# Queueing all loads of a convolution ahead of its stores, the last three as casting loads

## The chip, the cores and the metric

The kernel runs on one core of a Trainium2 chip. The metric is device time in microseconds (us), the median of several runs; the profiler's span of one execution, about 1.8 us shorter than the time of that same execution (127.3 us in one of 129.07 us), is used when stages are compared. All runs quoted with a verdict were in the fast state.

## The reference

A 3x3 convolution with padding 1, in fp32 in memory: 16 images of 64 channels and 64x64 pixels, 128 output channels.

```python
batch, c_in, h, w, c_out = 16, 64, 64, 64, 128
x_pad = np.pad(x, ((0, 0), (0, 0), (1, 1), (1, 1)))
output[b, co] += weight[co, ci, kh, kw] * x_pad[b, ci, kh:kh+h, kw:kw+w]   # over ci, kh, kw
```

The kernel must read 17.07 MB and write 33.55 MB.

## The kernel before

Two images form a pair: 2 x 64 channels fill 128 partitions. ScalarE casts the pair's fp32 input `xf` to fp16 (`xs`), GpSimd sums neighbouring rows (`ss`), TensorE makes three groups of products per block of 16 output rows, ScalarE copies the first group out of PSUM (`ut`), and VectorE adds it to the other two into the outputs `ot`. A pool named `big`, 16 KB per partition and buffer, serves inputs and outputs alike: a pair needs one buffer for `xf` and two for `ot`.

```python
psum = ctx.enter_context(tc.tile_pool(name="psum", bufs=8, space=bass.MemoryType.PSUM))
big = ctx.enter_context(tc.tile_pool(name="big", bufs=9))

def load(p):
    xf[p] = big.tile([128, H, W], F32, tag="big", name="xf")
    # ... nc.sync.dma_start(xf[p], x rows of pair p); pair 0 in four pieces

def outs(p):
    ots[p] = [big.tile([128, H // 2, 2, W], F32, tag="big", name="ot") for _ in range(2)]

for p in range(4):
    load(p)
outs(0)
# ... weights; casts and sums of pair 0
casts = {p: [[(p + 1, n)] for n in range(4)] for p in range(NP - 1)}   # pair p+1's casts during pair p
# ...
for p in range(NP):                       # NP = 8 pairs
    if p not in ots:
        outs(p)
    if p + 1 < NP:
        for lo in (0, 16):
            sums(nc.gpsimd, p + 1, xf[p + 1], lo, 16)
    for blk in range(4):
        U = group([(G1, None)])           # matmuls on ss
        # ScalarE: ut = copy of U (two tiles); then casts[p][blk]
        A = group([(G21, 1), (G0, -1)])   # matmuls on xs
        # VectorE: ots[p][b2][even rows] = A[b2] + ut[b2]
        Bt = group([(G01, 0), (G2, 2)])
        # VectorE: ots[p][b2][odd rows] = Bt[b2] + ut[b2]
        # after block 3 (pair 7: blocks 1 and 3): nc.sync.dma_start(out, ots[p][b2])
    if p < 4:
        load(p + 4)
        if p < 3:
            outs(p + 1)
```

Of the kernel before, what the change touches and what calls it, by code (L numbers as in the profile page):

```python
# [9 lines left out]
F16 = mybir.dt.float16  # L10


@with_exitstack
def kernel(
    ctx: ExitStack,
    tc: tile.TileContext,
    x: bass.AP,
    weight: bass.AP,
    out: bass.AP,
):  # L20
    nc = tc.nc
    B, CI, H, W = x.shape
    CO = weight.shape[0]
    assert H == 64 and W == 64 and CI == 64 and CO == 128 and B % 2 == 0
    NP = B // 2
    RB = 8

    keep = tc.keep_in_program_order
    x_rows = x.rearrange("b c h w -> (b c) h w")
    out_rows = out.rearrange("b co h w -> b co h w")  # L30
    w_flat = weight.rearrange("co ci kh kw -> co (ci kh kw)")

    const = ctx.enter_context(tc.tile_pool(name="const", bufs=1))
    psum = ctx.enter_context(tc.tile_pool(name="psum", bufs=8, space=bass.MemoryType.PSUM))
    xpool = ctx.enter_context(tc.tile_pool(name="xpool", bufs=3))
    big = ctx.enter_context(tc.tile_pool(name="big", bufs=9))
    spool = ctx.enter_context(tc.tile_pool(name="spool", bufs=3))
    upool = ctx.enter_context(tc.tile_pool(name="upool", bufs=4))




    w_raw = const.tile([CO, CI * 9], F32)
    nc.sync.dma_start(w_raw, w_flat)  # L44
    cuts = [(0, 18), (18, 34), (34, 50), (50, 64)]
    xf, xs = {}, {}

    def load(p):
        xf[p] = big.tile([128, H, W], F32, tag="big", name="xf")
        for lo, hi in cuts if p == 0 else [(0, H)]:  # L50
            keep(
                nc.sync.dma_start(
                    xf[p][:, lo:hi, :], x_rows[128 * p : 128 * p + 128, lo:hi, :]
                )
            )

    def cast(p, n):
        if p not in xs:
            xs[p] = xpool.tile([128, H, W], F16, tag="xs", name="xs")
        lo, hi = cuts[n]  # L60
        keep(nc.scalar.copy(xs[p][:, lo:hi, :], xf[p][:, lo:hi, :]))  # L61

    ots = {}

    def outs(p):
        ots[p] = [big.tile([128, H // 2, 2, W], F32, tag="big", name="ot") for _ in range(2)]

    for p in range(4):
        load(p)
    outs(0)  # L70
    ident = const.tile([128, 128], F16)
    make_identity(nc, ident)
    w16 = const.tile([CO, CI * 9], F16)
    keep(nc.vector.tensor_copy(w16, w_raw))  # L74


    ss = {}

    def sums(eng, p, src, lo, n):
        if p not in ss:  # L80
            ss[p] = spool.tile([128, H // 2, W], F16, tag="ss", name="ss")
        v = src.rearrange("p (j i) c -> p j i c", i=2)
        keep(
            eng.tensor_add(  # L84
                ss[p][:, lo : lo + n, :], v[:, lo : lo + n, 0, :], v[:, lo : lo + n, 1, :]
            )
        )


    Wt = const.tile([128, 5, 3, CO], F16)  # L90
    G0, G21, G1, G01, G2 = range(5)

    def wrow(i):
        return Wt[:, i, :, :].rearrange("p t c -> p (t c)")

    wps = {}
    for kh in (1, 2, 0):
        wp = psum.tile([128, 512], F32, tag="acc", name="wp")
        for k in range(3):
            t = 3 * kh + k  # L100
            for q in (0, 64):
                nc.tensor.matmul(wp[q : q + 64, k * CO : k * CO + CO], w16[:, t::9], ident)  # L102
        wps[kh] = wp[:, 0 : 3 * CO]
    keep(nc.scalar.copy(wrow(G1), wps[1]))  # L104
    sums(nc.vector, 0, xf[0], 0, RB)
    keep(nc.vector.tensor_sub(wrow(G21), wps[2], wrow(G1)))  # L106
    keep(nc.vector.tensor_sub(wrow(G01), wps[0], wrow(G1)))  # L107
    cast(0, 0)
    keep(nc.scalar.copy(wrow(G0), wps[0]))  # L109
    keep(nc.scalar.copy(wrow(G2), wps[2]))  # L110
    for n in range(1, 4):
        sums(nc.vector, 0, xf[0], RB * n, RB)


    casts = {p: [[(p + 1, n)] for n in range(4)] for p in range(NP - 1)}
    casts[0] = [[(0, 1)], [(0, 2), (0, 3)], [(1, 0), (1, 1)], [(1, 2), (1, 3)]]
    casts[NP - 1] = [[], [], [], []]

    for p in range(NP):
        if p not in ots:  # L120
            outs(p)
        if p + 1 < NP:
            for lo in (0, 16):
                sums(nc.gpsimd, p + 1, xf[p + 1], lo, 16)
        for blk in range(4):
            j0 = blk * RB

            def group(wi_rows):

                tiles = [  # L130
                    psum.tile([128, RB, W], F32, tag="acc", name="acc") for _ in range(2)
                ]
                n = 3 * len(wi_rows)
                i = 0
                for wi, off in wi_rows:
                    for kw in (1, 0, 2):
                        c_lo, c_hi = max(0, 1 - kw), min(W, W + 1 - kw)
                        for b2 in range(2):
                            p0 = 64 * b2
                            lo, hi = j0, j0 + RB  # L140
                            if off is None:
                                rhs = ss[p][p0 : p0 + 64, lo:hi, c_lo + kw - 1 : c_hi + kw - 1]
                            else:
                                while 2 * lo + off < 0:
                                    lo += 1
                                while 2 * (hi - 1) + off > H - 1:
                                    hi -= 1
                                first = 2 * lo + off
                                last = 2 * (hi - 1) + off
                                rhs = xs[p][  # L150
                                    p0 : p0 + 64,
                                    first : last + 1 : 2,
                                    c_lo + kw - 1 : c_hi + kw - 1,
                                ]
                            nc.tensor.matmul(  # L155
                                tiles[b2][:, lo - j0 : hi - j0, c_lo:c_hi],
                                Wt[p0 : p0 + 64, wi, kw, :],
                                rhs,
                                start=i == 0,
                                stop=i == n - 1,  # L160
                            )
                        i += 1
                return tiles

            U = group([(G1, None)])
            us = []
            for b2 in range(2):
                ut = upool.tile([128, RB, W], F32, tag="ut", name="ut")
                keep(nc.scalar.copy(ut, U[b2]))  # L169
                us.append(ut)  # L170
            for q, n in casts[p][blk]:
                cast(q, n)
            A = group([(G21, 1), (G0, -1)])
            for b2 in range(2):
                nc.vector.tensor_add(ots[p][b2][:, j0 : j0 + RB, 0, :], A[b2], us[b2])  # L175
            Bt = group([(G01, 0), (G2, 2)])
            for b2 in range(2):
                nc.vector.tensor_add(ots[p][b2][:, j0 : j0 + RB, 1, :], Bt[b2], us[b2])  # L178
            parts = {3: (0, 64)} if p < NP - 1 else {1: (0, 32), 3: (32, 64)}
            if blk in parts:  # L180
                lo, hi = parts[blk]
                for b2 in range(2):
                    keep(nc.sync.dma_start(
                        out_rows[2 * p + b2, :, lo:hi, :],
                        ots[p][b2].rearrange("p j i c -> p (j i) c")[:, lo:hi, :],
                    ))

        if p < 4:
            load(p + 4)
            if p < 3:  # L190
                outs(p + 1)


# [1 line left out]
_INS = ['x', 'weight']  # L195
# [26 lines left out]
```

## Time and profile before

| | before |
|---|---|
| time | 128.8 us (128.3 to 129.51, 3 runs) |
| span | 127.3 us |
| TensorE ends | 113 us |
| last data packet ends | 125.9 us |
| moved | 50.63 MB at 428 GB/s in the steady stretch |

A page shows the span in 40 equal slices of about 3.2 us. A digit is the busy share of an engine in tenths, 9 meaning full. Waits are listed as "engine, what it was about to write, line <- releaser: total us, times, longest". The lines that carry the reading of before stand in the prediction below.

### The profile page before, as it was taken

The page shows a single profiled execution, that of the slowest core. Times are in us where ns is not written, and L with a number is a line of the kernel's source. Part 1 is how long each engine was busy: PE and PEld are TensorE (multiplying, and loading weights), DVE is VectorE, ACT ScalarE, POOL GpSimd, SP SyncE. Part 2 cuts the span into 40 slices and gives each one's busy share as a digit, 9 for nine tenths or more (in the row PEclk, how much of TensorE's full clock was granted, in tenths as well). Part 3 has the DMA queues.
Part 4 walks back from the last instruction along what each step waited for, and adds up shares of the span by engine and source line. Part 5 has one row for each costly group of instructions (what it writes and reads, how often), then busy time and mean ns, then how long its engine had stood idle before and what let it go on. Part 6 is the DMA issues. An engine that isn't in the chain of part 4 may idle for free.

```text
span 127.3 us, 2440 instructions
## 1 busy us (share of the span) xinstructions
PE 108.7 (85%) x978; PEld 60.2 (47%) x978; DVE 84.2 (66%) x135; ACT 67.2 (53%) x100; POOL 33.5 (26%) x20
## 2 busy tenths in 40 slices
PE   0489999999999999999999999999999999990000
PEld 0334555564556655565556555555555555540000
DVE  0286777875778677777778678777877778773000
ACT  4283889866566646664666466666666633330000
POOL 2000399695000670009400390007600000000000
PEclk9999999999999999999999999999999999999555
DMA  4999999999999999999999999999999999999970
GB/s 127 300 427 438 432 427 427 391 417 412 350 422 355 430 427 409 443 427 417 427 432 438 422 417 422 453 422 427 422 417 448 422 422 427 450 391 430 425 337 18
DMA packets 4330, 50.77 MB, mean 399 GB/s; under 512 B 480, under 2 KB 480, under 8 KB 1120
## 3 DMA queue, kind: packets, MB, share of 16 engines
q1 hardware_dynamic: 4320, 50.63, 95.7%
q8 instruction: 7, 0.11, 0.3%
q14 instruction: 3, 0.02, 0.0%
HBM read 17.07 MB, written 33.55 MB: 398 GB/s over the span
## 4 chain that ended last, share of the span: by engine, by line
PE 75%; ACT 5%; issue 4%; DMA 4%; DVE 2%; DVEq 0%; SPq 0%
PE acc L155 75%; DMA xf<-in_x_dram 4%; ACT xs L61 3%; ACT ut L169 2%; DVE ot L175 1%; DVE ss L84 1%; DVE ot L178 0%; DVEq L217 0%; SPq L44 0%; DVEq L175 0%
## 5 line engine op out<-in xcount | busy, mean ns | idle before, releaser
L155 PE MATMUL acc<-xs,Wt 64*128 64x504 f16 (+3 forms) x768 | 102.9, 380 | 0.3
L155 PEld LDWEIGHTS <-Wt 64*128 64x128 f16 x960 | 59.1, 96 | 49.6 <-issue 6.5
L175 DVE TENSOR_TENSOR ot<-acc,ut 128x512 f32<-128x512 f32 x64 | 41.2, 686 | 24.4 <-PE acc L155 23.1
L169 ACT COPY ut<-acc 128x512 f32<-128x512 f32 x64 | 34.4, 590 | 40.9 <-issue 37.1
L84 POOL TENSOR_TENSOR ss<-xf 128x1024 f16<-128x1024 f32 x14 | 32.8, 2362 | 57.2 <-DMA xf<-in_x_dram 55.8
L155 PE MATMUL acc<-ss,Wt 64*128 64x504 f16 (+1 forms) x192 | 41.4, 384 | 1.4 <-DVE ss L84 1.4
L178 DVE TENSOR_TENSOR ot<-acc,ut 128x512 f32<-128x512 f32 x64 | 41.1, 684 | 0.7 <-PE acc L155 0.7
L61 ACT CAST xs<-xf 128x1024 f16<-128x1024 f32 (+2 forms) x32 | 33.5, 1058 | 0.8 <-DMA xf<-in_x_dram 0.8
L102 PE MATMUL wp<-ident,w 128*64 128x128 f16 x18 | 1.3, 328 | 4.2 <-DVE w L74 4.2
L84 DVE TENSOR_TENSOR ss<-xf 128x512 f16<-128x512 f32 x4 | 2.8, 690 | 2.7 <-DMA xf<-in_x_dram 2.7
L102 PEld LDWEIGHTS <-w 128*64 128x64 f16 x18 | 1.1, 209 | 4.2 <-DVE w L74 4.2
L74 DVE CAST w<-w_raw 128x576 f16<-128x576 f32 x1 | 0.5, 460 | 3.6 <-DMA w_raw<-in_weight_dram 3.6
L104 ACT CAST Wt<-wp 128x384 f16<-128x384 f32 x1 | 0.5, 479 | 2.8 <-PE wp L102 2.8
L104 ACT ACT_TABLE_LOAD x1 | 1.3, 1283 | 0.7 <-PEq L206 0.7
L109 ACT CAST Wt<-wp 128x384 f16<-128x384 f32 x1 | 0.5, 478 | 0.5 <-DVE Wt L107 0.5
L106 DVE TENSOR_TENSOR Wt<-wp,Wt 128x384 f16<-128x384 f32 x1 | 0.6, 552 | 0.0
L107 DVE TENSOR_TENSOR Wt<-wp,Wt 128x384 f16<-128x384 f32 x1 | 0.5, 549 | 0.0
L110 ACT CAST Wt<-wp 128x384 f16<-128x384 f32 x1 | 0.5, 485 | 0.0
masks.py:199 POOL TENSOR_SCALAR_AFFINE_SELECT ident<-ident 128x128 f16<-128x128 f16 x1 | 0.3, 292 | 0.1
masks.py:197 POOL MEMSET ident<- 128x128 f16 x1 | 0.2, 204 | 0.3 <-POOLq L206 0.3
L206 POOL MEMSET const-float32-0.0<- 128x1 f32 x1 | 0.1, 98 | 0.2 <-issue 0.2
L206 POOL MEMSET const-bfloat16-1.0<- 128x1 bf16 x1 | 0.1, 101 | 0.0
(2 smaller groups left out, 0.2 us busy)
## 6 DMA issues: line engine op xcount, KB each, us to landing
out_dram<-ot SPq DMA_DIRECT2D x14, 2048.0 KB, 13.6
xf<-in_x_dram SPq DMA_DIRECT2D x7, 2048.0 KB, 19.5
out_dram<-ot SPq DMA_DIRECT2D x4, 1024.0 KB, 10.6
xf<-in_x_dram SPq DMA_DIRECT2D x2, 512.0 KB, 6.1
xf<-in_x_dram SPq DMA_DIRECT2D x1, 576.0 KB, 4.9
xf<-in_x_dram SPq DMA_DIRECT2D x1, 448.0 KB, 7.1
w_raw<-in_weight_dram SPq DMA_DIRECT2D x1, 288.0 KB, 2.9
```

The source lines that it names most:

```text
L61: keep(nc.scalar.copy(xs[p][:, lo:hi, :], xf[p][:, lo:hi, :]))
L74: keep(nc.vector.tensor_copy(w16, w_raw))
L84: eng.tensor_add(ss[p][:, lo : lo + n, :], v[:, lo : lo + n, 0, :], v[:, lo : lo + n, 1, :])
L102: nc.tensor.matmul(wp[q : q + 64, k * CO : k * CO + CO], w16[:, t::9], ident)
L104: keep(nc.scalar.copy(wrow(G1), wps[1]))
L106: keep(nc.vector.tensor_sub(wrow(G21), wps[2], wrow(G1)))
L107: keep(nc.vector.tensor_sub(wrow(G01), wps[0], wrow(G1)))
L109: keep(nc.scalar.copy(wrow(G0), wps[0]))
L155: nc.tensor.matmul(tiles[b2][:, lo - j0 : hi - j0, c_lo:c_hi], Wt[p0 : p0 + 64, wi, kw, :], rhs, start=i == 0, stop=i == n - 1,)
L169: keep(nc.scalar.copy(ut, U[b2]))
L175: nc.vector.tensor_add(ots[p][b2][:, j0 : j0 + RB, 0, :], A[b2], us[b2])
L178: nc.vector.tensor_add(ots[p][b2][:, j0 : j0 + RB, 1, :], Bt[b2], us[b2])
```

## The change

The intent is that no store stands in front of a load. Pairs 0 to 4 are loaded as fp32 into eight buffers shared with the outputs, and pairs 5 to 7 by loads that cast on the way, issued from GpSimd into fp16 tiles of their own, so that ScalarE's casts for them vanish.

```diff
-    big = ctx.enter_context(tc.tile_pool(name="big", bufs=9))
+    big = ctx.enter_context(tc.tile_pool(name="big", bufs=8))
+    NH = 5
...
+    def load_cast(p):
+        xs[p] = xpool.tile([128, H, W], F16, tag="xc", name="xc")
+        keep(nc.gpsimd.dma_start(xs[p], x_rows[128 * p : 128 * p + 128, :, :]))
+
-    for p in range(4):
+    for p in range(NH):
         load(p)
     outs(0)
...
-    casts = {p: [[(p + 1, n)] for n in range(4)] for p in range(NP - 1)}
+    casts = {p: [[]] * 4 for p in range(NP)}
     casts[0] = [[(0, 1)], [(0, 2), (0, 3)], [(1, 0), (1, 1)], [(1, 2), (1, 3)]]
-    casts[NP - 1] = [[], [], [], []]
+    casts[1] = [[(2, 0), (2, 1)], [(2, 2)], [(2, 3), (3, 0)], [(3, 1)]]
+    casts[2] = [[(3, 2), (3, 3)], [(4, 0)], [(4, 1), (4, 2)], [(4, 3)]]
...
-                sums(nc.gpsimd, p + 1, xf[p + 1], lo, 16)
+                sums(nc.gpsimd, p + 1, xf[p + 1] if p + 1 < NH else xs[p + 1], lo, 16)
+        if p == 0:
+            for q in range(NH, NP):
+                load_cast(q)
...
-        if p < 4:
-            load(p + 4)
-            if p < 3:
-                outs(p + 1)
```

## The prediction

> **What bounds the kernel now.** I read the page's slices first, because they show which resource is full and when. The columns are 40 slices of 3.2 us; digits are tenths.
>
> ```profile
> span 127.3 us, 2440 instructions
> ...
> PE   0489999999999999999999999999999999990000
> ...
> DMA  4999999999999999999999999999999999999970
> GB/s 127 300 427 438 432 427 427 391 417 412 350 422 355 430 427 409 443 427 417 427 432 438 422 417 422 453 422 427 422 417 448 422 422 427 450 391 430 425 337 18
> DMA packets 4330, 50.77 MB, mean 399 GB/s; under 512 B 480, under 2 KB 480, under 8 KB 1120
> ```
>
> Two rows are at 9 nearly throughout, TensorE and DMA. TensorE stops near 114 us; the DMA row stays full for about 10 us more. So the end is set by the stores that are still queued when the arithmetic is over. The windows make that exact (columns: busy us of each engine, granted clock, DMA share, GB/s):
>
> ```profile
> 22.00:24.00 2.00, 2.00 (x22) 1.15 (x20) 1.70 (x3) 1.69 (x3) 2.00 (x1) 1.00 0.77 328
> ...
> 32.00:40.00 8.00, 8.00 (x79) 4.35 (x76) 6.55 (x12) 4.35 (x7) 0.00 (x0) 1.00 1.00 358
> 40.00:112.00 72.00, 71.80 (x663) 40.40 (x659) 55.03 (x89) 41.30 (x64) 18.74 (x8) 1.00 1.01 428
> ...
> 116.00:122.00 6.00, 0.00 (x0) 0.00 (x0) 0.00 (x0) 0.00 (x0) 0.00 (x0) 0.65 1.02 430
> ```
>
> For 72 us the transfers run at 428 GB/s, with loads and stores mixed, and at 430 when only stores are left. Direction and mixture thus make no visible difference. In the packet records a 16 KB packet takes 611 ns (median) on one DMA engine, 26.8 GB/s, times 16 is 429. The kernel must move 17.07 MB in and 33.55 MB out; 50.63 MB over 16 engines is 193 packets of 16 KB each, 193 x 0.611 = **118 us** of transfer. It begins at 1.9 us and the last engine's last packet ends at 125.9. The 6 us beyond 1.9 + 118 are: the small first packets (about 320 GB/s in 2 to 8 us, so 1.5 us), the gap at 22 to 24 us (0.5), two bursts of slow packets near 33 and 38 us (358 instead of 428 for 8 us, so 1.3), and one engine that also fetches instructions and ends 2 to 3 us after its neighbours.
>
> TensorE is the near second. Its waits and the DMA queue's own waits:
>
> ```profile
> PE wp L102 <- DVE w L74: 4.2, 1, 4.2
> PE acc L155 <- DVE ss L84: 1.4, 1, 1.4
> ```
>
> ```profile
> SPq L183 <- DVE ot L178: 97.4, 17, 18.0
> SPq L217 <- DMA out_dram<-ot: 9.6, 3, 4.8
> ```
>
> After the start TensorE never waits; each pair takes 13.35 us (stores of pairs 0, 1, 2, 3 are issued at 23.13, 36.60, 49.95, 63.29). The last line is the end of the program, waiting 9.6 us for stores. The last two were issued from 115.05 on. With an empty queue they would need about 4.9 us of transfer (2 x 1 MB; 16 packets of 8 KB per engine x 309 ns) and, from the gap between issue and first packet at the start, about 1.2 us before that: 115.9 + 1.2 + 4.9 = 122. So TensorE's own floor is near 122, against 125.9 now. **Only about 4 us can be won from the DMA side before TensorE binds.**
>
> **What the Trainium skill says.** "DMA: Bandwidth & Descriptors", section "Where 436 GB/s comes from", gives 435 GB/s for 16 ports of 256 bits at 850 MHz. The trace agrees: 428 to 430 held for 80 us. Its section "Issuing engines are not separate DMA queues" says that transfers issued from different engines run on the same 16 DMA engines and interleave. So a second queue brings no bandwidth; the trace of before has only one queue for data and can't show it. Its section "SWDGE vs HWDGE vs iDMA" says that a cast during a DMA must be issued from GpSimd, with descriptors computed there in software, in packets of preferably at most 4096 bytes. I found no figure for what a cast costs a DMA engine; this trace has none either. That is the main unknown.
>
> **The change, part by part.**
>
> 1. *Twelve casts leave ScalarE* (pairs 5 to 7, four each). The row `L61 ACT CAST` has 32 with a mean of 1058 ns (pieces 0.95 to 1.17), so about 12.5 us of ScalarE's 67. All of it lay beside TensorE, which did not wait for it: worth 0.
>
> 2. *The casts of pairs 2 to 4 move earlier*, six in pair 1 and six in pair 2 instead of four. A block lasts 13.35 / 4 = 3.34 us; with two casts ScalarE has 1.07 (two copies) + 2.0 = 3.1 us of work. It fits, as in pair 0, where the same density made TensorE wait for nothing. Worth 0, unless a load is late (rival 3).
>
> 3. *Loads of 4 to 7 are issued earlier.* Pair 4 is queued at the start. The casting loads come on GpSimd after its sums for pair 1, which ran from 14.66 to 19.36 us. So from about 20 us until about 2 + 17.07 / 0.429 = 42 us the loads run, stores of pair 0 (ready at 23.1) going in between or behind. Afterwards there are only stores: 33.55 / 0.429 = 78 us. Do they ever run dry? Each pair makes 4.19 MB, 9.8 us, every 13.35 us. By 42 us two pairs are ready; stored back to back they end near 52, 62, 71, 81, 91, 101, 111, and pair k's outputs are ready at 23.1 + 13.35 k: 90 for pair 5 and 103 for pair 6. Its transfer would begin at 101 to 103, so the queue just about runs dry at pair 6 and not before. It is then TensorE's floor of 122 that matters, and both limits nearly coincide. Output slots: pair 4 reuses pair 0's, needed from 64 us, stored by about 52. Pair 5 needs pair 1's at 77, stored by 62. No wait.
>
> 4. *The bytes.* Reads from memory stay at 17.07 MB, writes at 33.55. Only the on-chip side of three loads shrinks, 6.3 MB to 3.15. If an engine takes as long as its read side, 3 x 128 rows x 16 KB still cost 3 x 8 x 0.611 = 14.7 us. Smaller packets cost little: 4096 bytes take 159 ns here, 636 per 16 KB, so 4% of 14.7 = 0.6 us more.
>
> 5. *The gap at 22 to 24 us goes*, because pair 4's load is already queued: gain 0.5 us.
>
> Sum with the cast at its input's price: 127.3 + 0.6 - 0.5, and perhaps 0.5 to 1 less if the slow bursts near 33 and 38 us have to do with where loads and stores alternate. The span comes out at 126.5 to 127.5 and the time, 1.5 us above the span here, at 128 to 129.
>
> **The rivals.**
>
> *1. The cast is cheap: an engine takes as long as its write side.* Then 7.3 us of DMA work vanish, and TensorE's floor binds: last packet near 122 instead of 125.9, a time of about 125, 3% faster. For it: the narrow side is where the skill puts the port limit. Against: stores and loads run at one speed here, which looks like the engine's own rate, not that of a side.
>
> *2. The cast is dear*, by conversion or by descriptors made in software. At one and a half times its input's price it adds 7.3 us, at twice 14.7, all on the bound that ends last: 135 to 142. Nothing in the trace speaks against it; for the plain price speaks only that packet overhead is small for the sizes seen.
>
> *3. TensorE starves in pairs 1 to 3.* Two queues share the engines from 20 us. At half each, pair 3's load, 24.3 us in before, lands near 30 (2.1 MB at 214 GB/s from 20), and pair 4's near 40. Their first casts are due at about 31.5 and 41 in ScalarE's order. That is met by a hair; and ScalarE's copies out of PSUM stand behind a late cast. A cast queue that gets more than half would delay pair 4 by a few us, TensorE perhaps by 1 to 3 us (its eight banks cover some 2 us), and push the last store by as much. If packets take turns, 16 KB against at most 4 KB, the plain queue gets the larger part and nothing is late.
>
> *4. GpSimd is held up making descriptors*, and its sums for pair 2 come late. They were done at 24.2 us and are needed at 36.5: 12 us of slack, so hidden.
>
> **Range and chances.** The middle case (same bytes, same end) has most of the weight, the cheap cast gives about 125, and the dear one or starvation gives 131 and more, with a long tail. I take 127.8 us, with 125.2 to 132 for 8 in 10. Faster by over 2% (below 126.2): 0.24. Within 2%: 0.56. Slower by over 2% (above 131.4): 0.20.
>
> **What would show it.** Right: DMA row at 9 to about 122 or later, slices near 428 GB/s in 22 to 42 us too, 18 stores still queued behind one another at 113 us, the program's end waiting some 7 to 10 us for stores, and TensorE without a wait after 7 us. Packets of the casting queue would tell step 4: their time per byte read against 611 ns per 16 KB. Wrong towards fast: that ratio near one half, DMA share below 0.95 after 100 us. Wrong towards slow: the ratio well above 1, or TensorE zeros or waits for ScalarE in pairs 1 to 3, or waits of the vector adds on stores in pairs 4 to 7. The thinnest step is the price of a casting packet.

## The result, and the profile after

The changed kernel took 133.99 us (132.98 to 134.97, 4 runs) against 128.6 us for the kernel before beside it. The ratio is 1.0406, interval 1.0312 to 1.05. (A ratio here is the mean time of one kernel's fast runs over that of the other's in the same rounds, so not quite the ratio of the medians.) The prediction was 127.8 us, with 125.2 to 132 for 8 chances in 10: wrong, and on the slow side.

The slices of the changed kernel's page:

```profile
span 132.2 us, 2428 instructions
...
PE   0389999999992059999999999999999999997000
...
DMA  4999999999999999999999999699469937999992
```

TensorE has a hole at slices 12 to 14 (counted from 0; a slice is 3.3 us here, so about 40 to 50 us), and the DMA row, full to that point and well beyond, gets holes of its own later. The order in time says which came first. The waits of the changed kernel over the whole span:

```profile
ACT ut L178 <- DVE ot L187: 10.3, 1, 10.3
DVE ot L184 <- DMA out_dram<-ot: 9.1, 1, 9.1
PE acc L164 <- DVE ot L184: 7.3, 1, 7.3
```

These are three ends of one event, each happening once. VectorE waits 9.1 us for a *store* before it may write an output tile; TensorE waits for VectorE to empty PSUM; ScalarE waits behind them. The chain that ended last (start, length, what) and VectorE's timeline put it on the clock:

```profile
23.10 23.77 DMA out_dram<-ot
46.86 0.03 issue
...
46.99 0.70 DVE ot L184
47.69 0.04 issue
47.73 72.28 PE acc L164 x638
```

```profile
37.20 0.69 DVE L184 TENSOR_TENSOR ot<-acc,ut 128x512 f32<-128x512 f32 x1 [0.72 <-PE acc L164]
46.99 0.69 DVE L184 TENSOR_TENSOR ot<-acc,ut 128x512 f32<-128x512 f32 x1 [9.10 <-DMA out_dram<-ot]
```

The first line is the first image of pair 2, block 0; the second is the second image of the same block. The store it waits for was issued at 23.10 us: pair 0's first. That store took 23.8 us to land. What held it up is in the queues of the changed kernel and in the windows of the stall and after it:

```profile
q1 hardware_dynamic: 3888, 44.34, 80.4%
q0 software_dynamic: 432, 3.15, 11.4%
```

```profile
44.00:48.00 4.00, 0.27 (x2) 0.13 (x3) 1.01 (x2) 0.00 (x0) 0.00 (x0) 0.57 1.04 315
...
92.00:96.00 4.00, 4.00 (x41) 2.06 (x38) 3.27 (x6) 1.07 (x2) 0.00 (x0) 1.00 0.48 201
...
108.00:112.00 4.00, 4.00 (x42) 2.05 (x38) 3.40 (x6) 1.07 (x2) 0.00 (x0) 1.00 0.59 250
```

Queue q0 holds the casting loads. In the packet records a casting packet (16 KB read, 8 KB written) takes 624 ns on its DMA engine, and runs between 23.9 and 54.4 us. During the stall the DMA engines are full (share 1.04; 315 GB/s is counted because a casting packet counts by what it writes). So the engines did not idle; the plain queue had only about half of them. Half an engine's time is one 16 KB packet per 611 + 624 ns, or 212 GB/s over 16 engines, and that is all that the rest of the plain loads and pair 0's stores had. The packet records agree: between 24 and 44 us the plain queue moved 210 GB/s, with 260 casting packets beside its 256. Late in the run it is the reverse: TensorE is 7 us late, its stores come late, and the DMA engines run dry (shares 0.48 and 0.59).

The books close. From the starts of ScalarE's copies, pair 1 is 0.67 us shorter than before (12.81 against 13.48), pair 2 is 8.74 longer (22.08 against 13.34), pairs 3 and 4 are 0.54 shorter each. The sum is +7.0 us, and TensorE ends at 120.0 instead of 113.0. The last data packet ends at 130.6 instead of 125.9, +4.7: the remaining 2.3 us are put down to the backlog that before still had in its queue when TensorE was done. The span grew by 4.9.

Why does pair 2 wait for pair 0's store? The built program tells which semaphore each add waits for. The SyncE queue's transfers use eight semaphores in turn; counting them, number 5 and number 6 are the loads of pairs 1 and 2, and numbers 1 and 2, in their second use, are pair 0's two stores. The first adds of pairs 2 and 3 in the built changed kernel:

```
24 ot<-acc,ut [waits PE,DMAHW5,Activation,Pool]     pair 2, first image:  the buffer that held pair 1's input
25 ot<-acc,ut [waits DMAHW1,PE,Activation]          pair 2, second image: the buffer that pair 0's first store reads
33 ot<-acc,ut [waits DMAHW2,PE,Activation]          pair 3, first image:  the buffer that pair 0's second store reads
34 ot<-acc,ut [waits PE,DMAHW6,Activation,Pool]     pair 3, second image: the buffer that held pair 2's input
```

The pool does not hand out its eight buffers in turn; these waits fit an order of release as the program is written: pair 1's input has its last use within pair 0, then pair 0's outputs are released by the lines that *issue* their stores, and pair 2's input follows later, in pair 1. A buffer that is released on paper at 23 us and really free at 47 was preferred to one that is free in good time.

The choice itself is not new, which I overlooked: in the built kernel before, too, pair 2's second output has the buffer of pair 0's first, and the add waits for semaphore number 0 in its second use, that store's. But there the store landed at 30.3 us, and the add was due at 38.5 us:

```profile
37.90 1.29 DVE L175 TENSOR_TENSOR ot<-acc,ut 128x512 f32<-128x512 f32 x2 [0.72 <-PE acc L155]
```

Both images' adds run back to back (x2). So the change did not make the dependence; it used up some 8 us of slack in it. The fifth load ahead of the store takes part of that (the store lands at 35.9 us in e2 below, still in time), and the sharing with the casting loads the rest and more (46.9 us).

### The profile page after: what moved, and what is told of

Its sections match the earlier page's. It is cut to its first block, busy times and chain, and to the rows that moved or that the text cites. A ratio compares the mean times of both kernels' runs of the same rounds, so it can differ in the third digit from the quotient of the medians.

```text
span 132.2 us, 2428 instructions
## 1 busy us (share of the span) xinstructions
PE 108.4 (82%) x978; PEld 55.3 (42%) x978; DVE 84.1 (64%) x135; ACT 55.9 (42%) x88; POOL 33.8 (26%) x23
## 4 chain that ended last, share of the span: by engine, by line
PE 63%; DMA 22%; DVE 3%; ACT 2%; issue 1%; DVEq 1%; SPq 0%
PE acc L164 63%; DMA out_dram<-ot 18%; DMA xf<-in_x_dram 4%; DVE ot L184 2%; ACT xs L62 1%; DVE ot L187 1%; DVE ss L89 1%; DVEq L221 0%; ACT ut L178 0%; SPq L45 0%; DVEq L184 0%
## 5 line engine op out<-in xcount | busy, mean ns | idle before, releaser
L164 PEld LDWEIGHTS <-Wt 64*128 64x128 f16 x960 | 54.1, 96 | 61.6 <-issue 13.5
L164 PE MATMUL acc<-xs,Wt 64*128 64x504 f16 (+3 forms) x480 | 63.2, 385 | 7.4 <-DVE ot L184 7.3
L164 PE MATMUL acc<-ss,Wt 64*128 64x504 f16 (+1 forms) x192 | 36.1, 392 | 1.5 <-DVE ss L89 1.5
L164 PE MATMUL acc<-xc,Wt 64*128 64x504 f16 (+3 forms) x288 | 35.0, 373 | 0.0
L89 POOL TENSOR_TENSOR ss<-xf 128x1024 f16<-128x1024 f32 x8 | 18.8, 2369 | 20.1 <-DMA xf<-in_x_dram 14.0
L62 ACT CAST xs<-xf 128x1024 f16<-128x1024 f32 (+2 forms) x20 | 20.4, 1058 | 0.9 <-DMA xf<-in_x_dram 0.9
L89 POOL TENSOR_TENSOR ss<-xc 128x1024 f16<-128x1024 f16 x6 | 12.6, 2128 | 30.3 <-issue 30.3
L71 POOL DMA_DIRECT2D xc<-in_x_dram x3 | 1.8, 599 | 0.0
```

The source lines that it names most:

```text
L62: keep(nc.scalar.copy(xs[p][:, lo:hi, :], xf[p][:, lo:hi, :]))
L71: keep(nc.gpsimd.dma_start(xs[p], x_rows[128 * p : 128 * p + 128, :, :]))
L89: eng.tensor_add(ss[p][:, lo : lo + n, :], v[:, lo : lo + n, 0, :], v[:, lo : lo + n, 1, :])
L164: nc.tensor.matmul(tiles[b2][:, lo - j0 : hi - j0, c_lo:c_hi], Wt[p0 : p0 + 64, wi, kw, :], rhs, start=i == 0, stop=i == n - 1,)
```

## The experiments

Theory S: the slot wait, lengthened by the sharing of the DMA engines, is the whole loss. Rival D: casting loads, or two queues, cost the DMA engines more. Rival theories on smaller points are named with the runs.

### e1: the buffers strictly in turn

```diff
-    big = ctx.enter_context(tc.tile_pool(name="big", bufs=8))
+    big = ctx.enter_context(tc.tile_pool(name="big", bufs=1))
...
-        xf[p] = big.tile([128, H, W], F32, tag="big", name="xf")
+        xf[p] = big.tile([128, H, W], F32, tag=slot(), name="xf")    # "s0" ... "s7", "s0", ...; the outputs likewise
```

(GpSimd's sums are also written ahead of `outs(p)`.)

> The change with the eight shared slots taken strictly in turn (eight tags, one buffer each), so that pair 2's second output goes into pair 2's input slot and not into the slot whose store (pair 0, first image) is still queued; GpSimd's sums are written ahead of the slot request. Loads, casts and queues as in the changed kernel. Theory S (a vector add waits for a slot that a queued store holds, 9.1 us, and TensorE 7.3 us with it): the wait goes, TensorE ends near 113 us, time 127 to 129, ratio to before 0.99 to 1.01. Rival D (casting loads or two queues cost the DMA engines the time): stays at 132 or more.

Measured: 127.97 us (20 runs), ratio 0.992, interval 0.9894 to 0.9945. The wait is gone, with the casting loads exactly where they were. Its page and the main piece of its chain:

```profile
PE   0479999999999999999999999999999999920000
...
DMA  4999999999999999999999999999999999999960
```

```profile
7.25 102.89 PE acc L170 x948
```

TensorE runs through in one piece and ends at 110.1 us (113 expected; see e7 for the difference). Pair 0's first store still lands only at 46.4 us (46.6 in the changed kernel): the same late store harms nobody, because nobody waits for it. Theory S holds and rival D falls: the same casting loads on the same two queues, some 6 us faster.

### e2, e3, e4: how many casting loads go early

The buffers stay as in the changed kernel; none, one or two of the three casting loads are issued at pair 0, the rest at pair 3.

```diff
-        if p == 0:
-            for q in range(NH, NP):
+        if p == 0 or p == 3:
+            for q in range(NH, NH + n) if p == 0 else range(NH + n, NP):   # n = 0, 1, 2
                 load_cast(q)
```

> Slots as in the changed kernel, but all three casting loads are issued two and a half pairs later (after GpSimd's sums for pair 4, near 41 us), so pair 0's stores are behind five plain loads only and share with nothing. Theory S: pair 0's first store lands near 36 us instead of 46.9, before the add needs it at 37.9; no wait of TensorE, time 127 to 129. Rival D: the same casting work is still there, 132 or more.

> One casting load early, two near 41 us. By the sharing seen (16 KB of plain packet at 611 ns for each casting packet at 624 ns), 9.9 us of sharing: pair 0's first store lands near 41 us, the vector add waits about 3 us, TensorE about 1.5, time 128.5 to 130.5. Rival D: 132 or more as with three.

> Two casting loads early, one near 41 us. From the first casting packet at 23.9 us the plain queue has 4.2 MB left up to the end of pair 0's first store, 16 packets per engine, and two casting loads are 16 packets per engine: the whole stretch is shared, as with three. So store landing near 46 us, add waits about 9 us, TensorE about 7, time 132.5 to 135: the third casting load adds nothing. If the damage were in proportion to the casting loads it would be 132 or so with a wait of 6 us.

| early casting loads | pair 0's first store lands | add waits | TensorE waits | time | ratio to before |
|---|---|---|---|---|---|
| 0 (e2) | 35.4 us | 0 | 0 | 127.62 us | 0.990 |
| 1 (e3) | 39.9 us | 1.6 us | 0 | 127.69 us | 0.9919 |
| 2 (e4) | 44.8 us | 6.4 us | 4.6 us | 132.87 us | 1.0317 |
| 3 (the changed kernel) | 46.6 us | 9.1 us | 7.3 us | 133.99 us | 1.0406 |

(The landing is when the last of the 16 DMA engines posted its completion in the packet records; the semaphore of that landing, used in the text above, comes 0.3 to 0.5 us later. The last row is from another series; its ratio is to its own runs of before.) The adds in question, of e3 and then of e4, on VectorE's timeline:

```profile
40.36 0.69 DVE L184 TENSOR_TENSOR ot<-acc,ut 128x512 f32<-128x512 f32 x1 [1.55 <-DMA out_dram<-ot]
```

```profile
45.29 0.69 DVE L184 TENSOR_TENSOR ot<-acc,ut 128x512 f32<-128x512 f32 x1 [6.36 <-DMA out_dram<-ot]
```

The landing times were foretold within 1.2 us (36, 41, 46 expected), so the rule of sharing in equal turns carries. Two expectations missed. For e3 I had TensorE waiting 1.5 us and a time of 128.5 to 130.5; a wait of 1.6 us on VectorE reached TensorE not at all. With three and with two early loads TensorE's wait is 1.8 us shorter than the add's (9.1 and 7.3, 6.4 and 4.6), so the products already waiting in PSUM's eight banks hide about that much. For e4 I had said that the third casting load adds nothing; it adds another 1.8 us of landing and 2.7 us of wait on TensorE. By the mean of the 16 engines the third load costs the store only 0.7 us (44.5 us against 43.8). But the store is complete only with its slowest engine, which posts 2.3 us after the mean with three early loads and 1.4 us with two, probably because it is then still sharing; that reading was not tested by itself.

### e5: five loads ahead alone, without casting loads

The kernel before with its fifth load queued at the start and its nine buffers assigned by hand, so that no add waits for a queued store (the diff is cut; as in e1, GpSimd's sums are also written ahead of `outs(p)`).

```diff
+    xslot = "ABCDEAGH"
+    oslot = ["FG", "HI", "BC", "DF", "EI", "AB", "CD", "FG"]
...
-    for p in range(4):
+    for p in range(5):
         load(p)
...
-        if p < 4:
-            load(p + 4)
-            if p < 3:
-                outs(p + 1)
+        if p < 3:
+            load(p + 5)
```

> The kernel before with one part of the change alone: five plain loads instead of four at the start, no casting loads, the nine slots given by hand so that no add and no load waits for a store still queued. Theory Q (the 1% that the mended versions gain over before is the filled gap at 22 to 24 us and fewer slow packets, from having a load queued when the first stores are not ready): DMA share above 0.95 in 22 to 24 us, ratio to before 0.988 to 0.997. Rival C (the gain comes from the casting loads, by fewer ScalarE casts or fewer bytes written on chip): ratio 0.998 to 1.003 though the gap is gone.

Measured: 127.87 us, ratio 0.9921, interval 0.9895 to 0.9947, the same as e1, e2 and e3. No add waits for a store; two of the loads did, against the expectation, 4.7 us in all. So the 1% that the mended versions win over before comes from the fifth load ahead, and the casting loads add nothing visible. The windows of e5, to be held against those of before in the prediction:

```profile
22.00:24.00 2.00, 2.00 (x22) 1.05 (x20) 1.41 (x3) 1.79 (x3) 2.00 (x2) 1.00 0.96 410
...
32.00:40.00 8.00, 8.00 (x79) 4.13 (x76) 5.93 (x10) 5.71 (x9) 4.64 (x2) 1.00 1.00 426
```

Both weak stretches of before are gone, the gap at 22 to 24 us and the slow packets in 32 to 40. TensorE's pairs are shorter as well, 12.8 us. Which of these paid is told by the next run.

### e7: the PSUM banks strictly in turn, in the kernel before

In before, pairs 1 to 4 each have one block of 3.91 us (from copy to copy on ScalarE), 0.67 us more than in the changed kernel. The chain of before shows the place, once in each of those pairs:

```profile
42.80 0.59 ACT ut L169
43.40 0.04 issue
43.44 10.67 PE acc L155 x97
```

TensorE goes on when ScalarE has copied the block's own first product. That looks like a bank handed out too early, or like ScalarE being late because of its casts.

```diff
-    psum = ctx.enter_context(tc.tile_pool(name="psum", bufs=8, space=bass.MemoryType.PSUM))
+    psum = ctx.enter_context(tc.tile_pool(name="psum", bufs=1, space=bass.MemoryType.PSUM))
...
-                    psum.tile([128, RB, W], F32, tag="acc", name="acc") for _ in range(2)
+                    psum.tile([128, RB, W], F32, tag=bank(), name="acc") for _ in range(2)   # "b0" ... "b7", "b0", ...; wp of the weights likewise
```

> The kernel before with the eight PSUM banks taken strictly in turn (eight tags), nothing else. In before the blocks of pairs 1 to 4 have one of 3.91 us each, in the changed kernels 3.24; TensorE there resumes after ScalarE's copy of the same block's first product. Theory B (the bank assigned, not ScalarE's casts, makes that wait): all blocks near 3.24 us, TensorE ends near 110.5 us instead of 113; and since the DMA engines set the end, time unchanged, ratio 0.995 to 1.003. Rival (the casts on ScalarE make it): 3.91 blocks stay. Should TensorE be on the path, the ratio would be 0.98.

Measured: 128.96 us, ratio 0.9993, interval 0.9967 to 1.0018. The chain of e7 is one piece, and each pair takes 12.81 us although ScalarE casts exactly as before:

```profile
6.88 102.83 PE acc L161 x948
```

So the bank made the wait, not the casts. (The copies are not evenly spaced as I had expected: the 3.91 becomes 4.54 and the next 1.95, with the right sum.) TensorE ends at 109.7 us, 3.3 us earlier, and the time does not move: TensorE was off the path in before. The windows of e7:

```profile
22.00:24.00 2.00, 2.00 (x24) 0.99 (x21) 1.40 (x3) 2.00 (x3) 2.00 (x2) 1.00 1.01 434
...
32.00:40.00 8.00, 8.00 (x78) 5.97 (x76) 6.48 (x12) 5.62 (x9) 0.00 (x0) 1.00 1.00 360
```

Here the gap at 22 to 24 us is filled, since the first stores come a us earlier, and nothing is won that the runs can see (at most 0.4 us, by the interval). The slow stretch is still there, as in before. The gain of e5 is thus to be looked for in the slow packets: between 24 and 42 us, 27 packets over 1000 ns in before, 26 in e7, 3 in e5. The size fits: what all 16 KB packets took beyond 611 ns comes to 1.9 us per DMA engine in before, 1.8 in e7 and 0.8 in e5, and e5 gained about 1.0 us. Why packets are slow just there when pair 4's load is queued behind pair 0's stores stays open.

### e6: the same queue without a cast

One look, for the price of a packet: the kernel before, with the loads of pairs 5 to 7 issued from GpSimd as plain fp32.

```diff
-                nc.sync.dma_start(
+                (nc.gpsimd if p > 4 else nc.sync).dma_start(
```

> The kernel before with the loads of pairs 5 to 7 issued from GpSimd without a cast. For the price of the packet alone: 624 ns per 16 KB read in the casting loads against 611 in plain ones. If the cast costs the 13 ns, packets of this queue take 611; if the queue does, 624. The time is of no interest (GpSimd now waits for slots).

Measured: a packet of 16 KB takes 611 ns (median of 384) on this queue too, so the 13 ns of 624 are the cast's, 2%. The time is 131.67 us in the one run, whose state is unknown; the profile shows the same illness in another kernel:

```profile
q0 software_dynamic: 432, 6.29, 11.6%
```

```profile
DVE ot L175 <- DMA out_dram<-ot: 5.9, 1, 5.9
```

An add again waits for a store, here with no cast in the program. So the cast is not needed for the harm; this one look points to a second queue beside a store that someone waits for.

No version was tried that combines the hand-made buffers, the banks and late casting loads: the runs point to the DMA engines as the bound of each of the mended kernels (their last data packets end between 124.1 and 124.7 us, TensorE between 110 and 112), and none of these parts takes bytes away. e2 at 127.62 us and e5 at 127.87 us both beat the two kernels of the case, before by about 1%.

## Why the prediction was wrong

**The bound** was right: DMA engines first, TensorE near behind. e7 is the proof, 3.3 us of TensorE's time for nothing.

**The floor of TensorE was mis-sized.** I set it at 122 us from the last stores alone and concluded that about 4 us stood between the two limits. Pair 6's stores also come at its end: issued at 102.2 us in before, with 8.39 MB left from there (two pairs), 102.2 + 1.2 + 19.6 = 123 us. The room was 3 us, and 2.3 us of the delay were absorbed. The changed kernel confirms this working: there pair 6's stores were issued at 109.2 us onto an empty queue, 109.2 + 1.2 + 19.6 = 130.0, and the last packet ended at 130.6.

**The step that failed is part 3, the slots**, in the words: "Output slots: pair 4 reuses pair 0's, needed from 64 us, stored by about 52. Pair 5 needs pair 1's at 77, stored by 62. No wait." I assumed buffers in turn. The pool gave pair 2 the buffer of pair 0's first store, as it already did in before; it was needed at 37.9 us instead of 64. So the "No wait" became a wait of 9.1 us on VectorE and 7.3 us on TensorE. Its landing at 46.6 us was inside my own "by about 52"; had I read the built program's waits for the first adds of each pair, that one line would have given a wait of up to 14 us. The signs of being wrong did list adds that wait for stores, but in pairs 4 to 7. e1, which makes true what I assumed, gave 127.97 us against the 127.8 that I had predicted. That close a hit is partly luck, since small errors below cancel.

**The rivals.** Rival 3 (TensorE starves in pairs 1 to 3 because two queues share the engines) had the place and the mechanism of sharing, but the wrong victim: the loads of pairs 3 and 4 came in time (27.3 and 37.1 us, where 30 and 40 were foretold), and it was a store that came late. Its last sentence, that 16 KB packets against at most 4 KB would favour the plain queue, was wrong: the casting queue takes turns with whole rows, 16 KB read for 16 KB. Rivals 1 and 2 fell: the cast costs its input's time plus 2%, as the middle case had it (0.6 us in the sum; measured 24 packets per engine x 13 ns = 0.3 us). Rival 4 was as told: GpSimd spent 1.8 us on issuing and its sums came in time.

**The small terms.** The twelve removed casts were worth nothing in the time. TensorE's pairs did get shorter, by the banks, which I had not seen; e7 showed it worth nothing on the clock. The filled gap, for which I had counted 0.5 us, was worth nothing visible by itself (e7); the "perhaps 0.5 to 1" for the slow bursts was the part that came true (e5). A few readings were off without deciding anything: the time is 1.8 us above the span, not 1.5; the first data packet starts at 1.7 us, not 1.9; pair 3's load landed at 25.4 us in before, not 24.3; the last two stores were issued at 115.05 and 115.65 us, so the 115.9 stands in no record; and "18 stores still queued" at 113 us is the number of all stores (in e1, 5 of the 18 landed after 113 us). That the late DMA engine is the one that fetches instructions is not shown: the packet records do not name the engine.

## What to carry to other kernels

When a change alters a buffer pool that inputs and outputs share, or puts more transfers ahead of a store, read from the built program which buffer each tile gets, and for each buffer what it was last used for; a store's buffer is free when the store has landed, not where it was issued, and a pool may prefer it to one that is free sooner. In these runs a second DMA queue added no bandwidth (e6 moved 426 GB/s from 32 to 40 us with two plain queues busy, before 428 with one) and took an equal share of turns, so whatever waits in the first queue takes about twice as long while both are full (210 GB/s in place of 428). The advice of the Trainium skill ("Trainium Kernel Development and Optimization", section "Best Practices") that "consistent bubbles can mean SBUF/PSUM ran out" fits in part: before has one of 0.67 us in each of four pairs, but nothing had run out, since a different order of the same eight PSUM banks removed it (e7). The 9 us in the output buffer came once, and there too a buffer that would have been free in time existed (e1).

## What the Trainium skill lacked or had wrong

- "DMA: Bandwidth & Descriptors", section "SWDGE vs HWDGE vs iDMA", has no price for a cast. Here a casting load from fp32 to fp16 costs what it reads: 624 ns per 16 KB read and 8 KB written, against 611 ns for a plain 16 KB packet.
- The same section gives packets of preferably at most 4096 bytes. In this case's records the casting loads have one packet of 8192 bytes written per row, and plain loads from GpSimd one of 16,384. The casting packets alternate one for one with the other queue's 16 KB packets (260 to 256 between 24 and 44 us), and the plain queue fell from 428 to 210 GB/s.
- "Runtime: NRT & Kernel Launch", section "Instruction fetch mechanics", has the refills of the program's own instructions in blocks of 16 KB, but not what one costs a DMA engine: 7 packets of 16 KB at about 0.93 us each in before (611 ns for data of that size).
- No page that I read describes the slow stretch of before: 27 packets of over 1000 ns between 24 and 42 us, with 358 GB/s from 32 to 40 us, gone (3 packets, 426 GB/s) when one load was queued earlier. Its cause is open.
